# A streaming-encoder step: the last third of the projection moved into the attention's first tiles, and one chain of small passes for two DeltaNet tiles

## The chip, the cores and the metric

The kernel runs on one core of one Trainium2 chip. The metric is device time in microseconds (us); before the change three runs took 2844.42, 2846.88 and 2847.21 us (median 2846.88). Five engines work side by side, each on its own queue in order: TensorE (PE, with its weight loads as PEld), VectorE (DVE), ScalarE (ACT), GpSimd (POOL), and SyncE (SP), which here issues every DMA.

## The reference, cut to what matters

One layer of a streaming encoder over 2048 prompt frames and 8 running streams of 16 frames (17 tiles of 128 tokens). One input projection feeds three token mixers; an output projection, a layer norm and a feed-forward block follow.

```python
proj = jnp.einsum('btd,de->bte', x, lp['w_in'])
qa, ka, va, qkv_b, beta_in, a_in, gate_b, u_c = jnp.split(proj, split_points(IN_SIZES), axis=-1)
out_a = band_attention_prompt(qa, ka, va, lp['a_rel_bias'])     # softmax over 9 chunks of 64 keys
qb = l2_normalize(qb); kb = l2_normalize(kb)                    # x * rsqrt(sum(x*x) + 1e-6)
ob, s_new = gated_delta_rule(qb, kb, vb, g, beta, s0)           # group B, DeltaNet
ob = ob * lax.rsqrt(jnp.mean(ob * ob, -1, keepdims=True) + RMS_EPS) * lp['b_norm_w'] * gate
y_c, h_re, h_im = s5_ssm(u, ...)                                # group C, S5
mix = jnp.concatenate([out_a, out_b, out_c], axis=-1) @ lp['w_out']
x = layer_norm(DN_ALPHA * x + mix, lp['ln1_g'], lp['ln1_b'])
```

## The kernel before

Every float32 product of a projection is made of three matmuls of a rounded part and a rest (`mm3`, L64: high by high, low by high, high by low). Both parts come from `split` (L58): ACT casts, DVE subtracts.

The stages, in program order:

- **Projection 1** (`project1`, L263): the columns for S5, DeltaNet and the gates, half of the values, in three token parts, and keys, values and queries of the last 512 tokens and the streams.
- **Projection 2** (`project2_all`, L320): keys (two blocks of columns), second half of the values, queries (two blocks) for three blocks of 512 tokens: 15 steps. A step of keys or queries has 48 matmuls of 512 columns, the values' step 96 of 256 columns; one token block is 288 matmuls. Results go through a bank of `pps` (two), an ACT pass into `st` (two buffers), and a store to `kT`, `vS` or `qT` in DRAM.
- **DeltaNet** (`deltanet`, L166): tiles in pairs. For a tile `b_pre` runs the convolution, sums of squares `ss`, one reciprocal root by bit trick and three Newton rounds (`rsqrt`, L335: 12 DVE passes of 128x8), six factors `F`, and the products inside a chunk; `b_inverse` inverts the diagonal blocks of both tiles; then `b_solve`, `b_rec` (the state's recurrence) and `b_out`, which has a root of its own (12 passes of 128x4).
- **S5** (`s5`): eight steps with a round through DRAM each, then the gated output (`glw`).
- **Attention** (`attention`, L1070): setup, then 16 query tiles of four rounds (two heads each). Tile i looks at min(i+1, 5) key tiles, so the first tiles are short. A round is: scores on PE (`aps`), a DVE pass that adds the bias `nb` and takes the minimum, an ACT exponential, a DVE normalisation of `P`, transposes on PE into `tps` (three banks), copies to `PT`, and products with the values (`aob`). Tiles 1 to 8 also carry one running stream each (`sK`, `sV`).

`merge` (L121) interleaves generators: projection 2 at cost 1, DeltaNet at 1.0, S5 at 1.2 per step. Below that, a scheduler that models the engines orders each engine's instructions; a free engine takes what is ready, the earlier in the program first. With these paces DeltaNet and S5 are done when 10 of the 15 steps of projection 2 are, and the third token block (288 matmuls) runs with no partner. The attention's setup loads eight overlapping bias windows `rv` (L1084, two buffers, the tag `qd`) that ACT turns into `nb` (L1085); POOL then fills two corners (L1086, L1087). The query tile takes the same two buffers after them: `qd` (ACT, L1199, L1201) and its rest `qlz` (POOL, L1200).

Of the kernel before, what the change touches and what calls it, by code (L numbers as in the profile page):

```python
# [2 lines left out]

# [6 lines left out]
F32 = mybir.dt.float32  # L10
# [21 lines left out]
PACE1B = 1.25  # L32
PACE_B = 1.0
PACE_C = 1.2
KPITCH = 23 * 16

BLOCKS = ((0, 6), (6, 6), (12, 5))
# [4 lines left out]
class K:  # L42
# [31 lines left out]
    def run(self, upto=99):  # L74
        nc, A = self.nc, self.A
        with self.es:
            self.cst = self.pool("cst", 1)
            self.dram = self.pool("dram", 1, bass.MemoryType.DRAM)
            d = self.dram

            def parts(name, rows):
                return [d.tile([rows, T], F32, name=f"{name}{j}") for j, (_, T, _) in enumerate(PARTS)]

            self.bT = parts("bT", 768)
            TA = (512, 512, 512, 640)
# [12 lines left out]
            self.mixT = d.tile([1024, NT], F32, name="mixT")  # L98
            self.x1 = d.tile([NT, DM], F32, name="x1")
            self.x2 = d.tile([12 * 128, DM], F32, name="x2")  # L100
            self.wu0D = d.tile([7, 128, DM], F32, name="wu0D")
            self.ident = self.ld(self.cst, "c_ident")
            self.mix(upto)
            self.wes = ExitStack()
            self.w_load(self.wes)
            with ExitStack() as es:
                self.attention(es)
            if upto < 4:
                self.wes.close()
            if upto >= 4:  # L110
                with ExitStack() as fes:
                    self.w_out(fes)
                    if upto >= 5:
                        self.ffn(fes)
            for n in getattr(self, "debug", ()):
                o = A["dbg_" + n]
                t = getattr(self, n)
                nc.sync.dma_start(o, t[t.shape[0] - o.shape[0]:])
# [9 lines left out]
            except StopIteration:  # L128
                now.remove(s)

    def mix(self, upto):
        nc, A = self.nc, self.A
        bes, ses = ExitStack(), ExitStack()
        self.bp = self.pool("bp", 3, PSUM, es=bes, side="right")
        self.brp = self.pool("brp", 1, PSUM, es=bes, side="right")
        self.pp = self.pool("pp", 2, PSUM, es=ses)
        self.s5p = self.pool("s5p", 2, PSUM, es=ses)
        self.flip = 0
        self.parts_done = 0
        deltanet = self.deltanet()  # L140
        self.s5c = self.pool("s5c", 1, es=ses)
        with ExitStack() as es:
            dense = self.project1(es)
            next(dense)
            self.s5_setup()
            for _ in range(5):
                next(dense)
            self.parts_done = 1
            self.b_consts(bes)
            self.b_pools(bes)  # L150
            due = 0.0
            for i, _ in enumerate(dense):
                if i in (5, 11):
                    self.parts_done += 1
                due += PACE1 if i < 12 else PACE1B
                while due >= 1:
                    next(deltanet)
                    due -= 1
        with ExitStack() as es:
            self.merge((self.project2_all(es), 1.0), (deltanet, PACE_B), (self.s5(), PACE_C))  # L160
        nc.sync.dma_start(A["o_k"], self.kT[3])
        nc.sync.dma_start(A["o_v"], self.vS[3])
        ses.close()
        bes.close()

    def deltanet(self):  # L166

# [5 lines left out]
        for t in [0, 2, 4, 6, 8, 10, 16, 12, 14]:  # L173
            n = 1 if t == 16 else 2
            while not ready(t + n - 1):
                yield 0.1
            if gates < min(t // 6, 2):
                gates += 1
                self.b_gates(gates)
            blk = self.bw.tile([32 * n, 16, 16], F32, name="blk", tag="blk", bufs=2)  # L180
            st = []
            for i in range(n):
                st.append(self.b_pre(t + i, blk, i))
                yield 1
            TU = self.b_inverse(st, blk)
            for x, (T, U) in zip(st, TU()):
                self.b_solve(x, T, U)
                o = self.bw.tile([128, 1, 4, 64], F32, name="o", tag="o", bufs=2)
                if t == 16:
                    self.b_rec_sample(x, o)  # L190
                else:
                    self.b_rec([x], o)
                self.b_out(x["t"], 1, o)
                yield 1
        self.nc.sync.dma_start(self.A["o_sp"], self.S)

    def evac(self, dst, src, scale=None):
# [273 lines left out]
    def t2(self, name, tag="pa"):  # L471
        return self.bw.tile([128, 4, 128], F32, name=name, tag=tag, bufs=5 if tag == "pa" else 1)

    def b_pre(self, t0, blk, bi):

        nc, A = self.nc, self.A
        V, mm = nc.vector, nc.tensor.matmul
# [40 lines left out]
        elif t0 + n == 16:  # L518
            nc.sync.dma_start(A["o_cvp"], cv[:, :, 0])
        qk = bw.tile([128, n, 8, 64], F32, name="qk", tag="qk", bufs=2)  # L520
        ss = bw.tile([128, n * 8], F32, name="ss", tag="ss", bufs=2)
        R = []
        for i in range(n):
            t = t0 + i
# [9 lines left out]
            for f in range(2):  # L534
# [2 lines left out]
            V.tensor_tensor(r[:, :, 0:64], ps[:, 0:256].rearrange("p (h d) -> p h d", h=4),  # L537
                            self.hbeta[:, t].unsqueeze(2).to_broadcast([128, 4, 64]), OP.mult)
            R.append(r)
        V.tensor_scalar(ss, ss, 4e-6, None, OP.add)  # L540
        rn = self.rsqrt(bw, ss, n * 8, "bn").rearrange("p (t h) -> p t h", h=8)
        F = bw.tile([128, n, 6, 4], F32, name="F", tag="F", bufs=2)
# [4 lines left out]
        V.tensor_tensor(F[:, :, 3], F[:, :, 1], self.beta[:, tt], OP.mult)  # L547
        V.tensor_tensor(F[:, :, 4], F[:, :, 3], self.egc[:, tt], OP.mult)
        V.tensor_tensor(F[:, :, 5], F[:, :, 1], self.kd[:, tt], OP.mult)
        st = []  # L550
        for i in range(n):
            t = t0 + i
# [206 lines left out]
        for p in range(2):  # L759
            nc.sync.dma_start(A["o_ss"][:, p], Sc[p])  # L760

    def b_out(self, t0, n, o):

        nc = self.nc
        V = nc.vector
        bw, bp = self.bw, self.bp
        T = n * 128
        of = o.rearrange("p t h e -> p (t h) e")
        sq = bw.tile([128, n * 4, 64], F32, name="osq", tag="po", bufs=4)
        nc.gpsimd.tensor_tensor(sq, of, of, OP.mult)  # L770
        ms = bw.tile([128, n * 4], F32, name="ms", tag="ms", bufs=2)
        V.tensor_reduce(ms, sq, AX.X, OP.add)
        V.tensor_scalar(ms, ms, 1.0 / 64, 1e-6, OP.mult, OP.add)
        rn = self.rsqrt(bw, ms, n * 4, "on")
        V.tensor_tensor(sq, of, rn.unsqueeze(2).to_broadcast([128, n * 4, 64]), OP.mult)
        g = bw.tile([128, 2, T], F32, name="gt", tag="po", bufs=4)
        gsrc, gs = self.at(self.gT, t0)
# [292 lines left out]
    def attention(self, es):  # L1070
# [1 line left out]
        c = self.pool("ac", 1, es=es, side="right")  # L1072
        self.ak = self.pool("ak", 2, es=es, side="right")
        self.asp = self.pool("asp", 4, PSUM, es=es, side="right")
        self.sc = self.pool("sc", 1, es=es)
        self.sw = self.pool("sw", 1, es=es)
        self.aw = self.pool("aw", 2, es=es)
        self.atp = self.pool("atp", 3, PSUM, es=es)
        self.aop = self.pool("aop", 1, PSUM, es=es)
        nb = self.nb = c.tile([128, 8, 640], F32, name="nb", tag="nb")  # L1080
        r = A["relrev"]
        for h in range(8):
# [20 lines left out]
        t = self.a_tile(0)  # L1103
        for q in range(2):
            self.a_queries(t, q)


        rounds = []
# [3 lines left out]
        for i in range(16):  # L1112
# [3 lines left out]
            for p in range(4):  # L1116
# [31 lines left out]
                    self.s_turn(sample)  # L1148
                if p == 3 and i >= 8:
                    self.w_part(i - 8)  # L1150
            t = t1
            if i == 8:
                nc.sync.dma_start(self.mixT[0:512, SEQ:NT].rearrange("(f p) t -> p f t", p=128), self.sos)
# [6 lines left out]
        h, l = (w0[:, i].bitcast(F32R) for i in (1, 2))  # L1160
        self.w_in(0, w0[:, 0], self.y0, h, l)
        self.w_tile(0, self.y0, h, l, lambda: self.asp.tile([128, 512], F32, name="aps", tag="s"))

    def tsplit(self, parts, t):
        src, sl = self.at_a(parts, t)
# [74 lines left out]
    def a_turn(self, s):  # L1240
# [2 lines left out]
        units = s["units"] = [(q, j) for j in range(s["nk"]) for q in range(2)]  # L1243
        for u in range(0, len(units), 4):
            m = units[u:u + 4]
            ps = self.atp.tile([128, 512], F32, name="tps", tag="t")
            for k, (q, j) in enumerate(m):
                self.nc.tensor.transpose(ps[:, k * 128:(k + 1) * 128], P[:, q, j * 128:(j + 1) * 128], self.ident)
            src = ps[:, 0:len(m) * 128].rearrange("p (k t) -> p k t", t=128)
# [80 lines left out]
    def s_turn(self, s):  # L1330
        nc = self.nc
        P = s["P"]
        PT = s["PT"] = self.aw.tile([128, 10, 128], F32, name="sPT", tag="PT")
        ps = self.atp.tile([128, 512], F32, name="tps", tag="t")
# [3 lines left out]
        ps = self.atp.tile([128, 512], F32, name="tps", tag="t")  # L1338
# [15 lines left out]

    def s_out(self, b, s):

        ps = self.atp.tile([128, 512], F32, name="tps", tag="t")
# [577 lines left out]
```

## Time and profile before

| | us |
|---|---|
| median of three runs (2844.42 to 2847.21) | 2846.88 |
| the profiled execution | 2848.35 |
| its span | 2846.6 |
| PE busy | 2739.7 (96%) |
| DVE busy | 1947.2 (68%) |
| ACT, POOL busy | 1307.0, 1037.4 |

The span divides into projection 1 with DeltaNet (0 to 580), projection 2 with DeltaNet and S5 (to 867), projection 2 alone (to 918), attention (to 1205), and output projection and feed-forward. A busy time is the union of the instructions' durations; matmuls overlap, so their pitch is less than their duration. The PE clock of a stretch is a share of full speed.

### The profile page before, as it was taken

To read this page: it belongs to the slowest core of one execution; us is meant where nothing else is said; L and a number is where in the kernel's file an instruction comes from. 1 tells how busy PE (TensorE), PEld (TensorE's weight loads), DVE (VectorE), ACT (ScalarE), POOL (GpSimd) and SP (SyncE) were. 2 spreads that over 40 slices of the span, in tenths; PEclk is the share of its full clock that TensorE was granted. 3 is DMA by queue.
4 is the path that set the end of the run, shared out by engine and by line. 5 is a ranking of instruction groups with operands and counts; after the bars stand their busy time and mean duration, and the time that the engine had idled before them with its cause. 6 is when DMAs were issued, how large, how long until landed. Compare 5 with 4: busy or idle time off the path is not lost.

```text
span 2846.6 us, 46363 instructions
## 1 busy us (share of the span) xinstructions
PE 2739.7 (96%) x16685; PEld 2405.9 (85%) x16685; DVE 1947.2 (68%) x4949; ACT 1307.0 (46%) x2714; POOL 1037.4 (36%) x914
## 2 busy tenths in 40 slices
PE   8999999989989899999999999999999999999998
PEld 8988888867777677788889998989999988998897
DVE  7587888798653788878755555566556557676676
ACT  3554554343355778612334433454434335444443
POOL 0010111232221232122354454445544553676674
PEclk9999999999999999999999999999999999999999
DMA  5734445555457652156622211253222224422321
GB/s 183 208 106 118 116 114 125 151 147 155 146 147 244 207 168 61 51 199 203 231 88 65 84 60 60 74 207 119 74 74 90 89 67 165 155 91 94 119 87 55
DMA packets 293437, 355.55 MB, mean 125 GB/s; under 512 B 85699, under 2 KB 218647, under 8 KB 292887
## 3 DMA queue, kind: packets, MB, share of 16 engines
q1 hardware_dynamic: 293206, 352.59, 39.6%
q8 instruction: 131, 2.15, 0.3%
q14 instruction: 100, 0.81, 0.1%
HBM read 280.25 MB, written 74.89 MB: 125 GB/s over the span
## 4 chain that ended last, share of the span: by engine, by line
PE 71%; DVE 12%; DMA 6%; issue 4%; ACT 3%; POOL 3%; SPq 1%; DVEq 0%; ACTq 0%; POOLq 0%
PE fdp L66 8%; PE fdp L67 8%; PE fdp L65 8%; PE pps L66 3%; PE pps L67 3%; PE pps L65 3%; PE wops L65 2%; PE wops L67 2%; PE wops L66 2%; PE fupv L67 2%; PE fupv L65 2%; PE fupv L66 2%; PE fupz L67 2%; PE fupz L65 2%; PE fupz L66 2%
## 5 line engine op out<-in xcount | busy, mean ns | idle before, releaser
L1570 POOL TENSOR_TENSOR wu<-wur,wu 128x512 fp32r<-128x512 f32 x308 | 416.9, 1357 | 600.6 <-ACT wu L1569 599.6
L1693 DVE TENSOR_TENSOR fy<-fy,fdp 128x512 f32<-128x512 f32 x500 | 341.1, 685 | 255.8 <-PE fdp L67 255.6
L65 PE MATMUL fdp<-wdh,hh 128*128 128x512 f32 x1020 | 397.8, 391 | 1.6 <-DVE fy L1693 1.1
L67 PE MATMUL fdp<-wdh,hl 128*128 128x512 f32 x1020 | 397.3, 389 | 1.1 <-DVE hl L1643 1.1
L66 PE MATMUL fdp<-wdl,hh 128*128 128x512 f32 x1020 | 397.2, 389 | 0.8 <-DVE wdl L61 0.8
L1569 ACT CAST wu<-wur 128x512 fp32r<-128x512 f32 x308 | 189.5, 617 | 427.1 <-DMA wur<-in_w_upL 173.5
L65 PE MATMUL pps<-xh,wh 128*128 128x384 f32 (+2 forms) x800 | 280.4, 352 | 11.7 <-ACT xh L60 10.4
L66 PE MATMUL pps<-xl,wh 128*128 128x384 f32 (+2 forms) x800 | 279.9, 350 | 2.1 <-DVE xl L61 2.1
L67 PE MATMUL pps<-xh,wl 128*128 128x384 f32 (+2 forms) x800 | 277.6, 348 | 0.1
L65 PEld LDWEIGHTS fdp<-wdh,hh 128*128 128x128 f32 x1020 | 191.4, 188 | 42.0 <-DVE fy L1693 2.8
L67 PEld LDWEIGHTS fdp<-wdh,hl 128*128 128x128 f32 x1020 | 191.5, 188 | 41.8 <-DVE hl L1643 2.0
L66 PEld LDWEIGHTS fdp<-wdl,hh 128*128 128x128 f32 x1020 | 191.5, 188 | 39.0 <-DVE wdl L61 1.1
L1643 DVE TENSOR_TENSOR hl<-fre,hh 128x384 fp32r<-128x384 f32 (+1 forms) x180 | 145.4, 809 | 83.9 <-ACT hh L1642 83.0
L60 ACT CAST wdh<-wdr 128x1024 fp32r<-128x1024 f32 x92 | 96.6, 1051 | 204.4 <-PE fdp L67 202.7
L65 PEld LDWEIGHTS pps<-xh,wh 128*128 128x128 f32 x800 | 152.1, 191 | 24.9 <-ACT xh L60 12.8
L61 DVE TENSOR_TENSOR wl<-wr,wh 128x512 fp32r<-128x512 f32 (+1 forms) x152 | 107.2, 714 | 87.0 <-ACT wh L60 84.5
L66 PEld LDWEIGHTS pps<-xl,wh 128*128 128x128 f32 x800 | 152.1, 190 | 13.8 <-DVE xl L61 5.1
L67 PEld LDWEIGHTS pps<-xh,wl 128*128 128x128 f32 x800 | 152.1, 190 | 11.4 <-issue 1.8
L61 DVE TENSOR_TENSOR wdl<-wdr,wdh 128x1024 fp32r<-128x1024 f32 x92 | 131.6, 1436 | 11.0 <-ACT wdh L60 10.9
L60 ACT CAST wh<-wr 128x512 fp32r<-128x512 f32 (+1 forms) x152 | 92.4, 619 | 79.8 <-DMA wr<-in_w_inA 35.0
L1638 ACT ACTIVATE fre<-fre,ld_b_up 128x384 f32<-128x384 f32 (+1 forms) x144 | 86.0, 597 | 65.3 <-DVE fre L1647 43.0
L1229 ACT ACTIVATE P<-P,st 128x640 f32<-128x640 f32 (+4 forms) x128 | 97.2, 760 | 30.5 <-DVE st L1226 29.8
(577 smaller groups left out, 7250.7 us busy)
## 6 DMA issues: line engine op xcount, KB each, us to landing
wdr<-in_w_dnL SPq DMA_DIRECT2D x96, 512.0 KB
wur<-in_w_upL SPq DMA_DIRECT2D x88, 512.0 KB
wr<-in_w_inA SPq DMA_DIRECT2D x70, 512.0 KB
TU<-tD SPq DMA_DIRECT2D x34, 256.0 KB
y<-in_x SPq DMA_DIRECT2D x17, 512.0 KB
x<-y SPq DMA_DIRECT2D x17, 512.0 KB
fxr<-x SPq DMA_DIRECT2D x17, 512.0 KB
fy<-x SPq DMA_DIRECT2D x17, 512.0 KB
```

Source lines behind the costliest of these rows:

```text
L60: nc.scalar.copy(hi, src)
L61: nc.vector.tensor_tensor(lo, src, hi.bitcast(F32), OP.subtract)
L65: mm(out, lh, rh, start=first, stop=False, **kw)
L66: mm(out, lh, rl, start=False, stop=False, **kw)
L67: mm(out, ll, rh, start=False, stop=last, **kw)
L1229: self.nc.scalar.activation(x, x, AF.Exp, scale=-1.0, bias=st[:, q:q + 1], accum_out=st[:, 2 + q:3 + q])
L1569: self.nc.scalar.copy(hi, src)
L1570: P.tensor_tensor(lo, src, hi.bitcast(F32), OP.subtract)
L1638: nc.scalar.activation(r, src, AF.Relu, bias=self.bu[:, c * 2 + i:c * 2 + i + 1])
L1643: V.tensor_tensor(hl, r, hh.bitcast(F32), OP.subtract)
L1693: V.tensor_tensor(y, y, ps[x], OP.add)
```

## The change

In `mix` only the first 10 steps of projection 2 are merged with DeltaNet and S5. Their pools are then closed, the attention (now a generator that yields after its setup and after each round) is started, and each of the five steps left is followed by three attention rounds. The attention's pools all move to the right-hand side of SBUF, the transposes have one PSUM bank until projection 2 is done, then two more. In `deltanet` a tile's `b_pre` is cut into `b_conv`, `b_factors` (once for a pair, passes of 128x16) and the rest; `b_out` is cut into `b_square` (per tile), `b_root` (once for a pair) and the rest.

```diff
+PACE_A = 3
@@ mix
         with ExitStack() as es:
-            self.merge((self.project2_all(es), 1.0), (deltanet, PACE_B), (self.s5(), PACE_C))
+            dense = self.project2_all(es)
+            self.merge((itertools.islice(dense, 10), 1.0), (deltanet, PACE_B), (self.s5(), PACE_C))
+            sps.close()
+            bes.close()
+            cs.close()
+
+            next(attention)
+            for _ in dense:
+                for _ in range(PACE_A):
+                    next(attention)
         nc.sync.dma_start(A["o_k"], self.kT[3])
         nc.sync.dma_start(A["o_v"], self.vS[3])
         ses.close()
-        bes.close()
+        self.atps.append(self.pool("atq", 2, PSUM, es=self.aes))
+        self.w_load(self.wes)
+        for _ in attention:
+            pass
@@ deltanet
+            st, qr = [], []
+            ss = self.bw.tile([128, n * 8], F32, name="ss", tag="ss", bufs=2)
             for i in range(n):
-                st.append(self.b_pre(t + i, blk, i))
-                yield 1
+                qr.append(self.b_conv(t + i, ss[:, i * 8:(i + 1) * 8]))
+                if i < n - 1:
+                    yield 1
+            F = self.b_factors(t, n, ss)
+            for i in range(n):
+                st.append(self.b_pre(t + i, *qr[i], F[:, i:i + 1], blk, i))
+                if i < n - 1 or n == 1:
+                    yield 1
             TU = self.b_inverse(st, blk)
-            for x, (T, U) in zip(st, TU()):
+            os_ = []
+            ms = self.bw.tile([128, n * 4], F32, name="ms", tag="ms", bufs=2)
+            for i, (x, (T, U)) in enumerate(zip(st, TU())):
...
-                self.b_out(x["t"], 1, o)
-                yield 1
+                os_.append((o, self.b_square(o, ms[:, i * 4:(i + 1) * 4])))
+                if i < n - 1:
+                    yield 1
+            rn = self.b_root(n, ms)
+            for i, (o, sq) in enumerate(os_):
+                self.b_out(t + i, 1, o, sq, rn[:, i * 4:(i + 1) * 4])
+            yield 1
@@ b_square, b_root (new; b_out loses these lines)
+    def b_square(self, o, ms):
+        sq = self.bw.tile([128, 4, 64], F32, name="osq", tag="po", bufs=4)
+        of = o.rearrange("p t h e -> p (t h) e")
+        self.nc.gpsimd.tensor_tensor(sq, of, of, OP.mult)
+        self.nc.vector.tensor_reduce(ms, sq, AX.X, OP.add)
+        return sq
+
+    def b_root(self, n, ms):
+        self.nc.vector.tensor_scalar(ms, ms, 1.0 / 64, 1e-6, OP.mult, OP.add)
+        return self.rsqrt(self.bw, ms, n * 4, "on")
@@ attention, a_turn, s_turn, s_out
-        self.atp = self.pool("atp", 3, PSUM, es=es)
+        self.atps = [self.pool("atp", 1, PSUM, es=es, side="right")]
...
+    def turn_bank(self):
+
+        self.turns += 1
+        pool = self.atps[-1] if self.turns % 3 else self.atps[0]
+        return pool.tile([128, 512], F32, name="tps", tag="t")
```

The first place is SP, where S5's output has been stored (`mixT<-oc`) and the bias windows `rv` are loaded, with the stores of the third block's keys (`kT<-st`) and the weights (`wr`). Before:

```order
L1065 DMA mixT<-oc_10612 128x2176
L249 DMA kT_69<-st 128x512
L210 DMA wr<-in_w_inA 128x1024
L1084 DMA rv<-in_relrev 128x640
L249 DMA kT_69<-st 128x512
L1084 DMA rv<-in_relrev 128x640
L210 DMA wr<-in_w_inA 128x1024
```

After:

```order
L1110 DMA mixT<-oc_10252 128x2176
L276 DMA kT_69<-st 128x512 x2
L237 DMA wr<-in_w_inA 128x1024
L1132 DMA rv<-in_relrev 128x640 x2
L1333 DMA rvs<-in_relrev 16x528 x2
L1132 DMA rv<-in_relrev 128x640 x2
```

The first window still stands behind the second key store and a weight load; the eight windows now go out in pairs, with the streams' windows `rvs` between them and no store or weight.

The second place is PE, where the attention's first scores (`aps<-kst0,qd`) begin. Before:

```order
L66 MATMUL pps_11465<-xl70_11048,wh_11433 128x512
L67 MATMUL pps_11465<-xh70_11047,wl_11434 128x512
L1224 MATMUL aps_11628<-kst0_11563,qd_11605 128x192
L1225 MATMUL aps_11628<-kst0_11563,qlz0_11567 128x192
L1224 MATMUL aps_11633<-kst0_11563,qd_11605 128x192
```

After:

```order
L67 MATMUL pps_11209<-wl_11178,xh70_10798 128x256
L68 MATMUL pps_11209<-wh_11177,xl70_10799 128x256
L1280 MATMUL aps_10896<-kst0_10707,qd_10749 128x192
L1281 MATMUL aps_10896<-kst0_10707,qlz0_10711 128x192
L1280 MATMUL aps_10901<-kst0_10707,qd_10749 128x192
```

The first scores stood behind the last queries of the block (`pps` of 512 columns); now they stand behind its second value tile (256 columns), with 144 of the block's 288 matmuls still to come.

The third place is PE in tile 1, after its last scores of the second round (`aps<-kst0` with `qlz1`). Before:

```order
L1224 MATMUL aps_11785<-kst0_11563,qd_11669 128x256
L1225 MATMUL aps_11785<-kst0_11563,qlz1_11568 128x256
L1248 MATMUL tps_11800<-ld_c_ident_92,P_11749 128x128
L1336 MATMUL tps_11807<-ld_c_ident_92,sP_11727 128x128 x2
L1248 MATMUL tps_11800<-ld_c_ident_92,P_11749 128x128 x3
```

After:

```order
L1280 MATMUL aps_11129<-kst0_10707,qd_10937 128x256
L1281 MATMUL aps_11129<-kst0_10707,qlz1_10712 128x256
L66 MATMUL pps_11237<-wh_11163,xh00_10756 128x256
L67 MATMUL pps_11237<-wl_11164,xh00_10756 128x256
L68 MATMUL pps_11237<-wh_11163,xl00_10757 128x256
```

This is the first place at which matmuls of the projection (`pps`) stand among those of the attention; the last of the 144 stands just ahead of tile 3's first scores.

## Rows read from the trace of the kernel before

**Rows 1.** The page: busy time, share of the span and instructions of each engine.

```profile
PE 2739.7 (96%) x16685; PEld 2405.9 (85%) x16685; DVE 1947.2 (68%) x4949; ACT 1307.0 (46%) x2714; POOL 1037.4 (36%) x914
```

**Rows 2.** Windows: stretch, busy time (and count) by engine, PE clock, DMA.

```profile
140.00:760.00 620.00, 584.96 (x4303) 501.58 (x4302) 502.71 (x1894) 279.79 (x702) 126.73 (x189) 0.99 0.47 128
580.00:640.00 60.00, 47.41 (x337) 37.56 (x337) 55.31 (x194) 29.67 (x71) 25.24 (x30) 0.91 0.58 161
...
918.00:934.00 16.00, 11.49 (x66) 7.14 (x64) 9.25 (x44) 11.16 (x35) 5.38 (x8) 0.61 0.66 210
934.00:960.00 26.00, 23.86 (x245) 16.98 (x247) 17.37 (x70) 18.51 (x51) 4.55 (x9) 0.91 0.74 225
```

**Rows 3.** PE's waits from 140 to 760: sum, times, longest.

```profile
PE bps L535 <- DVE s L515: 4.9, 3, 3.8
PE bps L587 <- POOL qdkb L574: 4.4, 9, 2.0
PE bps L583 <- DVE qkn L572: 3.4, 4, 1.3
...
PE bps L583 <- DVE F L548: 0.6, 1, 0.6
...
PE brs L690 <- DVE vn L687: 0.3, 1, 0.3
```

**Rows 4.** Two of the small passes: count, shortest/median/longest ns.

```profile
L349 DVE TENSOR_TENSOR bns<-bns,bnh x51: 146/158/599, 137.0 to 664.3; 128x8 f32<-128x8 f32 x51
L349 DVE TENSOR_TENSOR ons<-ons,onh x51: 136/154/567, 206.2 to 759.2; 128x4 f32<-128x4 f32 x51
```

**Rows 5.** The same for a factor of F.

```profile
L548 DVE TENSOR_TENSOR F<-F,b_egc x17: 143/673/1026, 140.6 to 667.0; 128x4 f32<-128x4 f32 x17
```

**Rows 6.** DVE in order of time: start, duration, instruction.

```profile
204.14 0.16 DVE L345 TENSOR_SCALAR bnh<-ss 128x8 f32<-128x8 f32 x1
204.21 0.15 DVE L773 TENSOR_SCALAR ms<-ms 128x4 f32<-128x4 f32 x1
204.28 0.16 DVE L344 TENSOR_SCALAR bny<-bnt 128x8 int32<-128x8 int32 x1
```

**Rows 7.** PE in order of time, around the first scores; in brackets the idle before.

```profile
892.65 0.38 PE L65 MATMUL pps<-wh,xh 128*128 128x256 f32 x1 [0.89 <-ACT st L198]
...
918.14 0.25 PE L1224 MATMUL aps<-kst,qd 128*128 128x192 f32 x1
...
958.50 0.50 PE L1224 MATMUL aps<-kst,qd 128*128 128x512 f32 x1
```

**Rows 8.** SP in order of time: the first and third window.

```profile
874.52 0.57 SPq L1084 DMA_DIRECT2D rv<-in_relrev  x1
...
881.52 0.33 SPq L1084 DMA_DIRECT2D rv<-in_relrev  x1
```

**Rows 9.** ACT in order of time: four of the eight `nb`.

```profile
880.76 0.74 ACT L1085 ACTIVATE nb<-rv 128x640 f32<-128x640 f32 x1
...
886.63 0.74 ACT L1085 ACTIVATE nb<-rv 128x640 f32<-128x640 f32 x1 [0.52 <-DMA rv<-in_relrev]
...
897.38 0.74 ACT L1085 ACTIVATE nb<-rv 128x640 f32<-128x640 f32 x1 [3.09 <-DMA rv<-in_relrev]
...
905.57 0.74 ACT L1085 ACTIVATE nb<-rv 128x640 f32<-128x640 f32 x1 [2.90 <-DMA rv<-in_relrev]
```

**Rows 10.** SP: the sixth and seventh window's issue.

```profile
893.07 0.87 SPq L1084 DMA_DIRECT2D rv<-in_relrev  x2
```

**Rows 11.** POOL in order of time, the end of the setup.

```profile
906.37 0.52 POOL L1086 MEMSET nb<- 64x512 f32 x1 [90.33 <-ACT nb L1085]
906.92 0.52 POOL L1087 MEMSET nb<- 64x512 f32 x1
908.46 1.45 POOL L1200 TENSOR_TENSOR qlz<-qr,qd 64x512 fp32r<-64x512 f32 x1 [1.01 <-ACT qd L1199]
...
918.46 1.53 POOL L1279 TENSOR_SCALAR nbs<-rvs 128x528 f32<-128x528 f32 x1 [4.16 <-PE aps L1224]
```

**Rows 12.** Windows again, at the two stretches of half clock.

```profile
602.00:610.00 8.00, 4.88 (x12) 3.91 (x13) 7.90 (x16) 4.02 (x9) 3.99 (x4) 0.50 0.76 208
921.00:938.00 17.00, 13.25 (x72) 8.29 (x71) 9.34 (x40) 11.05 (x33) 3.69 (x7) 0.52 0.73 222
```

More of the change, by code (lines that the diff above doesn't have):

```diff
@@ L1 @@
-import math
+import itertools, math
 from contextlib import ExitStack
@@ L102, in run @@
             self.ident = self.ld(self.cst, "c_ident")
-            self.mix(upto)
             self.wes = ExitStack()
-            self.w_load(self.wes)
             with ExitStack() as es:
-                self.attention(es)
+                self.mix(upto, self.attention(es))
             if upto < 4:
@@ L129, in merge, with mix @@
                 now.remove(s)
-    def mix(self, upto):
+    def mix(self, upto, attention):
         nc, A = self.nc, self.A
@@ L136, in mix @@
         self.pp = self.pool("pp", 2, PSUM, es=ses)
-        self.s5p = self.pool("s5p", 2, PSUM, es=ses)
+        sps = ExitStack()
+        self.s5p = self.pool("s5p", 2, PSUM, es=sps)
         self.flip = 0
@@ L140, in mix @@
         deltanet = self.deltanet()
-        self.s5c = self.pool("s5c", 1, es=ses)
+        cs = ExitStack()
+        self.s5c = self.pool("s5c", 1, es=cs, side="right")
         with ExitStack() as es:
@@ L180, in deltanet @@
             blk = self.bw.tile([32 * n, 16, 16], F32, name="blk", tag="blk", bufs=2)
-            st = []
+            st, qr = [], []
+            ss = self.bw.tile([128, n * 8], F32, name="ss", tag="ss", bufs=2)
             for i in range(n):
-                st.append(self.b_pre(t + i, blk, i))
-                yield 1
+                qr.append(self.b_conv(t + i, ss[:, i * 8:(i + 1) * 8]))
[6 more added lines that the diff above has]
+                    yield 1
             TU = self.b_inverse(st, blk)
-            for x, (T, U) in zip(st, TU()):
+            os_ = []
+            ms = self.bw.tile([128, n * 4], F32, name="ms", tag="ms", bufs=2)
+            for i, (x, (T, U)) in enumerate(zip(st, TU())):
                 self.b_solve(x, T, U)
@@ L472, in t2, with b_conv @@
         return self.bw.tile([128, 4, 128], F32, name=name, tag=tag, bufs=5 if tag == "pa" else 1)
-    def b_pre(self, t0, blk, bi):
+    def b_conv(self, t0, ss):
         nc, A = self.nc, self.A
@@ L520, in b_pre @@
         qk = bw.tile([128, n, 8, 64], F32, name="qk", tag="qk", bufs=2)
-        ss = bw.tile([128, n * 8], F32, name="ss", tag="ss", bufs=2)
         R = []
@@ L539, in b_pre, with b_factors @@
             R.append(r)
+        return qk, R
+    def b_factors(self, t0, n, ss):
+        V, bw = self.nc.vector, self.bw
         V.tensor_scalar(ss, ss, 4e-6, None, OP.add)
@@ L549, in b_pre @@
         V.tensor_tensor(F[:, :, 5], F[:, :, 1], self.kd[:, tt], OP.mult)
+        return F
+    def b_pre(self, t0, qk, R, F, blk, bi):
+        nc = self.nc
+        V, mm = nc.vector, nc.tensor.matmul
+        n = 1
+        sam = t0 == 16
+        bw, bk, bp = self.bw, self.bk, self.bp
         st = []
@@ L760, in b_rec_sample, with b_out @@
             nc.sync.dma_start(A["o_ss"][:, p], Sc[p])
-    def b_out(self, t0, n, o):
+    def b_square(self, o, ms):
[7 more added lines that the diff above has]
+        return self.rsqrt(self.bw, ms, n * 4, "on")
+    def b_out(self, t0, n, o, sq, rn):
         nc = self.nc
@@ L768, in b_out @@
         of = o.rearrange("p t h e -> p (t h) e")
[L769 to L774, printed above, removed]
         V.tensor_tensor(sq, of, rn.unsqueeze(2).to_broadcast([128, n * 4, 64]), OP.mult)
@@ L1074, in attention @@
         self.asp = self.pool("asp", 4, PSUM, es=es, side="right")
-        self.sc = self.pool("sc", 1, es=es)
-        self.sw = self.pool("sw", 1, es=es)
-        self.aw = self.pool("aw", 2, es=es)
-        self.atp = self.pool("atp", 3, PSUM, es=es)
-        self.aop = self.pool("aop", 1, PSUM, es=es)
+        self.sc = self.pool("sc", 1, es=es, side="right")
+        self.sw = self.pool("sw", 1, es=es, side="right")
+        self.aw = self.pool("aw", 2, es=es, side="right")
+        self.aop = self.pool("aop", 1, PSUM, es=es, side="right")
+        self.aes = es
+        self.atps = [self.pool("atp", 1, PSUM, es=es, side="right")]
+        self.turns = 0
         nb = self.nb = c.tile([128, 8, 640], F32, name="nb", tag="nb")
@@ L1105, in attention @@
             self.a_queries(t, q)
+        yield
         rounds = []
@@ L1150, in attention @@
                     self.w_part(i - 8)
+                yield
             t = t1
@@ L1245, in a_turn @@
             m = units[u:u + 4]
-            ps = self.atp.tile([128, 512], F32, name="tps", tag="t")
+            ps = self.turn_bank()
             for k, (q, j) in enumerate(m):
@@ L1333, in s_turn @@
         PT = s["PT"] = self.aw.tile([128, 10, 128], F32, name="sPT", tag="PT")
-        ps = self.atp.tile([128, 512], F32, name="tps", tag="t")
+        ps = self.turn_bank()
         for j in range(4):
@@ L1337, in s_turn @@
         self.nc.scalar.copy(PT[:, 0:4], ps.rearrange("p (k t) -> p k t", t=128))
-        ps = self.atp.tile([128, 512], F32, name="tps", tag="t")
+        ps = self.turn_bank()
         self.nc.tensor.transpose(ps[0:16, 0:128], P[:, 512:528], self.ident)
@@ L1355, in s_out @@
     def s_out(self, b, s):
-        ps = self.atp.tile([128, 512], F32, name="tps", tag="t")
+        ps = self.turn_bank()
         self.nc.tensor.transpose(ps[:, 0:128], s["P"][:, 0:128], self.ident)
```

## The prediction

> **What bounds the kernel now.** I read the page's busy line first: PE is busy 2739.7 us of 2846.6 (96%), DVE 68% [rows 1]. So a change pays only where PE is idle, or where its clock is down. The windows show how much of that lies in the two stretches the change touches [rows 2]. In 140 to 760, where DeltaNet runs beside the projections, PE is busy 584.96 of 620: 35.0 us idle. DVE is busy 502.71, idle 117.3. In 580 to 640 inside it the clock is 0.91, which is 0.09 x 60 = 5.4 us lost, and DVE is busy 55.31 of 60. Where the attention begins, 918 to 934, PE is idle 4.5 us with a clock of 0.61; from 934 to 960 it is idle 2.1 us.
>
> Third, the waits of PE in 140 to 760. They begin with DVE's `s` (4.9 us) and end with `vn` (0.3). The 14 rows on DVE and the one on POOL's `qdkb` add up to 27.3 us. Of these the chain that leads through the factors `F` has three: `qdkb` 4.4, `qkn` 3.4, `F` 0.6, together 8.4 [rows 3].
>
> Last, the instructions in order of time around the attention's start: PE goes through the third token block without a hole until its first scores at 918.14 [rows 7], while SP, ACT and POOL prepare the bias beside it [rows 8 to 11]. That preparation is finished about 10 us before PE asks for it. So it costs nothing before the change, because 288 matmuls cover it.
>
> **Part B, the shared chains.** For each tile of a pair there were 1 + 12 passes for the root of `ss`, 6 for `F`, 1 + 12 for the root of `ms`: 32. A pair now makes one set: 8 pairs x 32 = 256 DVE passes go; the ones that stay are twice as wide. A small pass has a median of 154 to 158 ns [rows 4], a factor of `F` 673 ns [rows 5]. But passes that don't depend on each other start 0.07 us apart (204.14, 204.21, 204.28) although each lasts 0.15 to 0.16 [rows 6]. So I count 0.075 us each, and eight of the long `F` rows at the 0.6 that they hold the engine longer: 256 x 0.075 + 8 x 0.6 = 24 us of DVE freed. By durations it would be 256 x 0.155 = 40 us.
>
> DVE is not the bound, so freed time is no gain by itself. Bounds: below, nothing, since PE waits on DVE for other things; above, every idle microsecond of PE in the stretch and the clock too, 35.0 + 5.4 = 40. On the other side stands a new wait: both tiles' factors wait for the second tile's convolution and sums, so tile 0 of a pair starts its products later. I have no row of such a pair; the longest `qkn` wait is 1.3 us [rows 3], and eight pairs of that are +10. The value: half of the 8.4 us on the factors' chain goes (one of the two chains of a pair is left), −4.2. The rest of the waits, 27.3 − 8.4 = 18.9, and the 5.4 of clock, together 24.3, I let shrink as DVE's idle time grows: 24 on 117.3 is 20%, so −4.9. B = −9 us. It is nearer to 0 than to 40 because the waits that stay, on `s` above all, have no pass of these chains in their names.
>
> Rows 6 show these starts 0.07 us apart, and the sum goes by them. The Trainium skill, page "VectorE: DVE Perf Modes", section "The TRN2 errata — SBUF-src ops pay a fixed extra latency per instruction", says against this that each instruction pays a fixed latency between instructions, so that many small tiles pay it each time; its measured fixed term of about 150 cycles at 0.96 GHz is 0.156 us (an estimate by that page). By it the 256 passes would free 40 us and more, DVE's idle time would grow by a third, and B would be some −12 instead of −9. The durations of rows 4 agree with that price and the starts of rows 6 do not, where passes are independent; in a chain of dependent ones the duration counts.
>
> **Part A, the mixing.** No matmul goes or comes; 144 of the 288 of the third block move from in front of the first scores into tiles 1 and 2. They took 892.65 to 918.14 = 25.5 us [rows 7], and PE stood idle 0.89 before them, so the half that stays ahead ends at 892.65 − 0.89 = 891.8 (its start is set by S5's end and is left as it was). From there on PE has nothing until the first scores may start.
>
> When may they? All eight `nb`, the two corners of POOL, the windows of the streams and the query tile come first, since the query takes the two buffers that the windows had. Before, the windows went out at 874.52, 881.52, ... with stores and weights between them [rows 8], the `nb` ended 0.74 after 880.76, 886.63, 897.38, ..., 905.57 [rows 9], that is 906.3 for the last. A window that went out at 881.52 was read at 886.63, 5.1 us later [rows 8, 9]; one from 893.07 at 897.38, 4.3 [rows 9, 10]. Now the first still stands behind a store and a weight load, so `nb` 0 ends at 881.5 as before; then the windows go in pairs. The remaining turns of two buffers are three for windows 2 to 6 (a landing of 5.1, a pass of 0.74 and an allowance of 0.15 for the issue, 6.0 each): 881.5 + 18.0 = 899.5 for `nb` 6, and its partner at once behind, some 901 with the second pass and its wait for the shared queue. Behind that POOL's rows: two corners of 0.52 (now the last two stand behind each other), one pass of 1.53 for the streams' window, which stands ahead of `qlz`, and `qlz` of 1.45 [rows 11]: 1.0 + 1.5 + 1.5 = 4.0 from 901 is 905; the corners partly overlap the last pass, and I take 904. With landings of 4.3 it is 902.5; if the last `nb` comes at 906.3, as before, it is 910.3.
>
> So the new stall is 904 − 891.8 = 12.2 us. What it costs in the end is read at tile 3, from which on all is as before. Tile 3's first score was at 958.50, 40.4 us behind 918.14 [rows 7]. Now: 904 + 40.4 + 25.5 for the moved matmuls, less what they fill. They don't fill tile 0 and half of tile 1, as they stand on PE's queue behind the second round of tile 1; so of the idle 4.5 and 2.1 I count half or 3 us. 904 + 40.4 + 25.5 − 3 = 966.9, and 966.9 − 958.5 = +8.4. Bounds: with 902.5 and all 6.6 filled, +3.3; with 910.3 and 1 filled, +18.7. I take +8, for the row that it is nearest to is a landing of 5.1. The clock gives nothing back in this: 921 to 938 ran at 0.52, near the lower of the two levels, 1.2 GHz [rows 12], and a stall of 12 us comes ahead of the same tile now. That one transpose bank serves tiles 0 to 2 instead of three I cost at nothing, as those matmuls are few against the 25.5 us of dense ones that stand between; without that cover it is part of the upper bound.
>
> The stretch in which S5 ends gets the streams' two sample loads earlier, beside S5's own; I have no row that prices this and take 0.
>
> **Sum.** +8.4 − 9.1 = −0.7 us against the profiled 2848.35, which is 1.47 above the median 2846.88. Set against the median: 2846 us, no change. What counts as none is within 0.2%, 5.7 us, about what a measurement of this kernel can tell.
>
> **Rivals.** *Faster, by the dip at 602 to 610.* There the clock was 0.50 and PE busy 4.88 of 8 while DVE was busy 7.90 [rows 12], and all of 580 to 640 has DVE at 92% [rows 2]: here DVE is the bound. If freed passes undo this, its idle 12.6 us and the 5.4 of clock go nearly whole, and half the chain's waits (4.2) with them: B = −22. With A at +4 to +8 that is −14 to −18: about 2832. For it speaks that an engine at 92% with a queue in order turns each pass into delay; against it that the first of the waits, on `s`, is not on these chains. Chance 0.36.
>
> *Slower, by the setup.* The stall ahead of the first scores decides. If the windows come no faster than before (SP's queue still holds a store and a weight ahead of the first, and keys and values of the attention now land in the same microseconds), the last `nb` ends at 906.3, the scores begin at 910.3, the stall is 18.5 us and A = +15 to +18. With B at half its value, −4.5: +10 to +14, about 2859. It decides from A − B = 5.7 on, so with B = −9 from a first score at 910 on. For it speaks that SP issues in order, so that its first window waits where it did; against it that stores and weights have left the row of windows. Chance 0.26.
>
> *The mixing does nothing it says.* Half the block still stands in front, and the matmuls that were to fill tile 0 stand behind it, so A is only a shift of 25.5 us with a stall in its place. That is how I have it in the forecast; if the stall were filled as well, A = 0 and the time 2838, inside the faster side.
>
> **Chances.** Forecast (both terms within a few us of each other) 0.38, faster 0.36, slower 0.26. Its own range is 2841 to 2852; with the rivals' times 2832 and 2859, and a little of their own bounds, 2828 to 2862 holds 8 in 10. The extremes, B = −40 or A = +18.7 with B = +10, are left out.
>
> **What would show it.** A: PE idle of about 12 us between the last matmul of the values' second tile and the first score, named after `qlz`, `nb` or a window; first score at about 904 less what B gained by then; idle from there to tile 3 below 4 us outside the half clock. B: DVE some 24 us less busy in 140 to 760 (40 by durations), the rows on `F`, `qkn` and `qdkb` halved, PE's idle there at about 28 us. It is wrong if the stall is under 4 us, if 580 to 640 loses most of its 12.6 idle, or if new waits on tile 0's factors stand among the longest of PE.

## The result

The changed kernel took 2873.15 us (median of 4 runs, 2869.82 to 2880.28) against 2845.65 for the kernel before: ratio 1.0101, 95% interval 1.0086 to 1.0116, 27.5 us slower. (A difference here is that of the medians; a ratio is worked out from the single runs and can differ from it by a microsecond or two.) The forecast was 2846 with a range to 2862. It lies 11 us beyond the range, and 14 beyond the time of the slower rival. The profiled execution took 2880.28 us, the slowest of the four.

The page of the changed kernel, its first part (as [rows 1]):

```profile
PE 2751.1 (96%) x16685; PEld 2414.8 (84%) x16685; DVE 1939.6 (67%) x4693; ACT 1308.1 (45%) x2714; POOL 1039.5 (36%) x914
```

DVE has its 256 instructions less (4949 to 4693), and over the whole span that is 1947.2 − 1939.6 = 7.6 us of DVE, where the sum counted 24. The windows of the stretches of [rows 2]:

```profile
140.00:760.00 620.00, 571.44 (x4221) 492.17 (x4221) 477.76 (x1612) 270.44 (x685) 124.49 (x181) 0.98 0.44 122
580.00:640.00 60.00, 47.32 (x317) 37.41 (x317) 48.22 (x166) 27.55 (x66) 24.60 (x34) 0.91 0.44 133
```

From 140 to 760 PE is idle 48.6 us where it was 35.0, and its clock is 0.98 for 0.99: some 13.5 + 6 us lost. In 580 to 640 DVE is less busy (48.22 for 55.31), and PE's busy time (47.32 for 47.41) and clock are what they were. (The 25 us that DVE lacks in the long window are mostly not saved but late: the page's total fell by 7.6.)

Windows at the same times don't hold the same work: the long one has 4221 matmuls where it had 4303. The same work ends with S5's last gated matmuls (`glw`), before and after:

```profile
862.64 2.09 PE L1057 MATMUL s5p<-yq,glw 128*128 128x272 f32 x8
```
```profile
883.80 2.09 PE L1102 MATMUL s5p<-yq,glw 128*128 128x272 f32 x8
```

The windows up to there, before and after:

```profile
0.00:864.73 864.73, 806.23 (x5546) 703.31 (x5547) 655.93 (x2375) 397.75 (x952) 154.91 (x227) 0.99 0.51 144
```
```profile
0.00:885.89 885.89, 815.00 (x5550) 710.28 (x5551) 649.75 (x2120) 397.68 (x953) 158.70 (x231) 0.97 0.50 143
```

Of the 21.2 us more, 12.4 are idle time of PE (58.5 to 70.9) and 8.8 are matmuls that take longer, at a clock of 0.97 for 0.99.

PE's longest waits from 140 to 760, as [rows 3]:

```profile
PE s5p L1014 <- DVE WB L1009: 9.7, 1, 9.7
PE brs L831 <- DVE osq L820: 7.2, 6, 2.1
PE bqs L689 <- DVE R L701: 5.9, 9, 1.7
...
PE brs L776 <- DVE vns L784: 4.0, 1, 4.0
PE bps L623 <- DVE qkn L612: 3.0, 4, 0.9
...
PE bps L627 <- POOL qdkb L614: 0.6, 3, 0.2
```

The waits that the sum halved did shrink: `qdkb` from 4.4 to 0.6, `qkn` from 3.4 to 3.0, `F` from 0.6 to no row. What came instead has other names: the outputs' transposes (`osq`), the solve (`R`), the streams' recurrence (`vns`), S5 (`WB`). The wait on `WB` lies at 626, in the stretch 580 to 640, where PE's idle time is 12.7 us and was 12.6: there it takes the place of other waits and adds nothing.

The attention's start on PE, as [rows 7] (idle before in brackets), and tile 3's first score:

```profile
918.15 0.50 PE L1280 MATMUL aps<-kst,qd 128*128 128x192 f32 x1 [9.97 <-ACT qd L1257]
...
982.02 0.50 PE L1280 MATMUL aps<-kst,qd 128*128 128x512 f32 x1
```

The first score comes when it came before (918.14), with 144 matmuls still to do: S5's last gated matmuls came 21 us later. At tile 3 the lag is 982.02 − 958.50 = 23.5 us.

### The profile page after: what moved, and what is told of

Same layout as the page of the kernel before. It is cut to its first block, busy times and chain, and to the rows that moved or that the text cites. A ratio compares the mean times of both kernels' runs of the same rounds, so it can differ in the third digit from the quotient of the medians.

```text
span 2878.5 us, 46133 instructions
## 1 busy us (share of the span) xinstructions
PE 2751.1 (96%) x16685; PEld 2414.8 (84%) x16685; DVE 1939.6 (67%) x4693; ACT 1308.1 (45%) x2714; POOL 1039.5 (36%) x914
## 4 chain that ended last, share of the span: by engine, by line
PE 75%; DVE 10%; DMA 5%; issue 5%; ACT 4%; POOL 2%; SPq 1%; DVEq 0%; ACTq 0%; POOLq 0%
PE fdp L66 8%; PE fdp L67 8%; PE fdp L68 8%; PE pps L68 3%; PE pps L66 3%; PE pps L67 3%; PE fupv L68 2%; PE fupv L66 2%; PE fupv L67 2%; PE fupz L68 2%; PE fupz L67 2%; PE fupx L67 2%; PE fupx L68 2%; PE fupz L66 2%; PE fupx L66 2%
## 5 line engine op out<-in xcount | busy, mean ns | idle before, releaser
L68 PEld LDWEIGHTS pps<-xh,wl 128*128 128x128 f32 x800 | 152.4, 191 | 12.4 <-DVE wl L62 3.3
L225 ACT ACTIVATE st<-pps 128x384 f32<-128x384 f32 (+3 forms) x122 | 56.5, 466 | 119.3 <-PE pps L68 106.9
```

The lines of the kernel that those rows point to most:

```text
L68: mm(out, ll, rh, start=False, stop=last, **kw)
L225: self.nc.scalar.activation(dst, src, AF.Copy, scale=scale or 1.0)
```

## The experiments

Differences are against the kernel before on the same chip. "Order" and "slack", named in some expectations, are theories on the DeltaNet part that came up after the first four runs.

**1. The two halves apart.** DeltaNet's new functions in the kernel before:

```diff
-                st.append(self.b_pre(t + i, blk, i))
+                qr.append(self.b_conv(t + i, ss[:, i * 8:(i + 1) * 8]))
...
+            rn = self.b_root(n, ms)
```

> The kernel before with both shared chains and nothing else of the change. Theory 1 (the DeltaNet part of the change makes the loss ahead of the attention, the mixing the rest): +14 to +20 us against before, and S5's last gated matmul as late as in the changed kernel, some 21 us later than the 862.6 of before. Theory 2 (the loss ahead of the attention comes from the mixing: the pools on the other side and the sample loads beside S5): within 4 us of before. The prediction's own figure for this part was -9.

Measured +18.4 us (1.0059, 1.0046 to 1.0071). Next the changed kernel with the old DeltaNet functions (the same lines the other way).

> The changed kernel with the old DeltaNet code, so the mixing alone. Theory 1: +7 to +12 us against before (the prediction had +8), S5's last gated matmul within 3 us of before's 862.6, an idle stretch of PE of about 10 us ahead of the first score. Theory 2: +20 us or more, S5's end some 20 us late.

Measured +8.6 (1.0028, 1.0018 to 1.0037). S5's last gated matmuls, in the first and in the second:

```profile
880.67 2.09 PE L1092 MATMUL s5p<-yq,glw 128*128 128x272 f32 x8
```
```profile
865.50 1.08 PE L1077 MATMUL s5p<-yq,glw 128*128 128x272 f32 x4
```

The parts add up to 27.0 of 27.5: theory 1 holds. PE in the mixing alone, at the end of the dense half block, at the first scores and at tile 3's first score:

```profile
886.82 0.28 PE L68 MATMUL pps<-wh,xl 128*128 128x256 f32 x1
898.25 0.50 PE L1255 MATMUL aps<-kst,qd 128*128 128x192 f32 x1 [11.14 <-ACT qd L1232]
900.52 0.53 PE L1256 MATMUL aps<-kst,qlz 128*128 128x192 f32 x1 [1.78 <-POOL qlz L1231]
...
964.89 0.50 PE L1255 MATMUL aps<-kst,qd 128*128 128x512 f32 x1
```

12.9 us of stall in two rows; the sum had 12.2.

**2. The mixing's stall.** All eight windows land at once. Each has a place of its own, all loads go out ahead of the eight ACT passes, and the streams' windows behind them:

```diff
+        room = [nb[:, h + 4] for h in range(4)]
+        room += [self.aw.tile([128, 1024], F32, name="rv", tag="qd")[:, 0:640] for _ in range(2)]
+        rt = self.aw.tile([128, 10, 128], F32, name="rt", tag="PT").rearrange("p a b -> p (a b)")
+        room += [rt[:, 0:640], rt[:, 640:1280]]
-            rv = self.aw.tile([128, 1024], F32, name="rv", tag="qd")[:, 0:640]
+            rv = room[h]
...
+        for h in range(8):
+            rv = room[h]
```

> The mixing alone (old DeltaNet code), but the eight bias windows land in eight places (four in the slots of nb that are written later, two in the query's buffers, two in a PT buffer), so that no load waits for an earlier one. If the stall ahead of the first scores is made of the turns of two buffers and is what the mixing costs (+8.6): PE's idle there falls from 12.9 to under 5 us and the time to within 3 us of before. Rival (the moved matmuls fill nothing and cost themselves, whatever the stall): the stall shrinks but the time stays at +6 or more.

Measured −1.6 (0.9990, 0.9981 to 0.9999), 10 us below the mixing alone. The first score, and the last windows on SP (`rv`, `rt`):

```profile
890.39 0.33 PE L1261 MATMUL aps<-kst,qd 128*128 128x192 f32 x1 [1.74 <-ACT qd L1238]
```
```profile
873.57 1.13 SPq L1111 DMA_DIRECT2D rv<-in_relrev  x2
874.80 1.46 SPq L1111 DMA_DIRECT2D rt<-in_relrev  x2
```

So the turns of two buffers, with what was issued between them, were the stall. Yet with it gone the mixing gains only 1.6 us, and the interval barely excludes no change. One reason stands in tiles 4 to 8, from the same product with the values to the same: before, in the mixing alone, then here.

```profile
982.15:1091.25 109.10, 99.17 (x1053) 77.60 (x1052) 90.06 (x296) 82.89 (x185) 30.30 (x31) 1.00 0.48 149
```
```profile
989.29:1101.84 112.55, 100.02 (x1053) 78.01 (x1052) 94.13 (x297) 84.32 (x185) 29.60 (x31) 0.98 0.47 146
```
```profile
977.10:1092.10 115.00, 101.72 (x1054) 79.62 (x1053) 94.02 (x297) 84.26 (x185) 29.59 (x31) 0.97 0.46 143
```

The same matmuls take 5.9 us longer here, 3.4 in the mixing alone, at a lower clock. Why they do is open. Then `PACE_A` at 5:

> The mixing alone with the windows landing at once, and five attention rounds behind each of the five dense steps instead of three, so that the last dense matmuls fall into tiles 4 and 5, where PE was idle 10 us of 109. If dense work fills that idle time: 3 to 6 us below before. Rival (tiles 4 to 8 are paced by DVE at 90 us of 109 and the dense matmuls' own passes, and one transpose bank holds them longer): within 3 us of before, or slower.

Measured +3.5 (1.0013, 1.0003 to 1.0023), as the rival had it. Dense matmuls don't fill those tiles for free.

**3. Which chain.** One of the two shared at a time:

> The kernel before with the factors of a pair shared, the output's root per tile. Theory 1a (tile 0 of a pair starts its products only behind the second tile's convolution, which delays inverse and recurrence: waits on R, vn, vns): +8 to +18 us. Theory 1b (the shared root at the pair's end makes the loss): -6 to +3, the waits on osq as small as before (1 us).

> The kernel before with the output's root shared by a pair, the factors per tile. Theory 1b (both tiles' outputs wait for the second recurrence and one chain of small passes, and PE's transposes of osq stand in its queue meanwhile: 8.4 us of waits on osq in the changed kernel, 1.0 before): +8 to +18 us, with at least 6 us of waits on osq. Theory 1a: -6 to +3.

Factors alone (`b_conv`, `b_factors`, old `b_out`): +21.8 (1.0070, 1.0051 to 1.0088). Root alone (`b_square`, `b_root`, old `b_pre`): +14.0 (1.0041, 1.0029 to 1.0053). Both theories fail: one chain costs 21.8 or 14.0 where the two together cost 18.4, and PE's waits on `osq` from 140 to 867 are 9.4 us with the factors shared, where the root wasn't touched, and 7.9 with the root. The cause isn't in one chain.

**4. The order without the sharing, and the saving without the order.** The first edit, against the kernel with both chains shared:

```diff
-            F = self.b_factors(t, n, ss)
+            F = [self.b_factors(t + i, 1, ss[i]) for i in range(n)]
-            rn = self.b_root(n, ms)
+            rn = [self.b_root(1, m) for m in ms]
```

> The kernel before, with the DeltaNet steps cut and waiting as in the shared version (a pair's factors behind both convolutions, both outputs at the pair's end), but every tile keeps its own passes: nothing is shared, no pass is saved. Theory order (what costs is that the pair's work is moved together: the factors wait for the second tile, the outputs come in one lump with the next pair's inverse): +12 to +25 us, as the shared version (+18). Theory slack (what costs is that fewer passes are counted in the order that was written down, so that PE's transposes and products stand closer to the DVE passes they wait for than the chip can follow): at most +6.

Measured +17.4 (1.0059, 1.0046 to 1.0073), where the shared version had +18.4. No pass is saved and no tile waits for another's data. (Not shown above: the small passes have more buffers, two for each root's and four for `ss`, `ms` and `F`; `osq` of both tiles is held to the pair's end as in the shared version.) The program's order alone is enough for the cost. PE's waits on the factors in this kernel, 140 to 760:

```profile
PE bps L616 <- POOL qdkb L603: 2.7, 3, 2.2
...
PE bps L612 <- DVE qkn L601: 0.7, 2, 0.3
```

In the other run `range(3)` becomes `range(1)` in `rsqrt`:

> The kernel before with one Newton round instead of three in both reciprocal roots of DeltaNet: the last two rounds are left out, 12 DVE passes less per tile, 204 in all, and each chain about 1 us shorter; no step is moved. The prediction's reckoning of freed DVE time: -3 to -8 us. Theory slack: +5 to +15, with new waits on osq or F. Theory order: -5 to +2, waits on osq as small as before.

Measured +0.3 (1.0001, 0.9993 to 1.0010). Its page:

```profile
PE 2737.4 (96%) x16685; PEld 2400.7 (84%) x16685; DVE 1932.2 (68%) x4745; ACT 1306.5 (46%) x2714; POOL 1042.3 (37%) x914
```

15.0 us of DVE are freed, twice what the change freed, and the time stays. (Kernels with all 4949 passes lie between 1943.7 and 1951.8, so such differences are good to some microseconds.) Slack falls, and so does the reckoning behind half of part B: by the interval the gain is at most 2 us. Then one piece moved, tile 0's output behind the second recurrence:

```diff
-                self.b_out(x["t"], 1, o)
-                yield 1
+                outs.append((x["t"], o))
...
+            for to, o in outs:
+                self.b_out(to, 1, o)
```

> The kernel before, where the output of a pair's first tile is written behind the second tile's recurrence, with its own root: nothing shared, no new wait, one block of the program moved later. Theory order (the place of the outputs in the program costs, not the shared chain): +8 to +18, as the shared root alone (+14). Rival (only the wait of both outputs for one root costs): within 4 us of before.

Measured +14.9 (1.0051, 1.0036 to 1.0066): order again.

**5. Can other cuts mend it?** The shared chains with the `yield` between the convolutions moved behind the second tile's products, then with eight half steps (`PACE1`, `PACE1B` doubled, `PACE_B` halved):

> The kernel before with both shared chains, but the steps cut so that a pair's both convolutions, its factors and tile 0's products stand in the first step, as early as before; inverse and first recurrence begin the third step again. Theory order, in the form that the products stand too late in the program: 0 to +8. In the form that the outputs in one lump at the pair's end cost (the shared root alone cost +14): +10 to +16. Theory slack: +12 or more.

> Both shared chains, but a pair is cut into eight half steps at twice the pace, so that the dense matmuls are spread evenly over its pieces: convolution, convolution, factors and products of tile 0, products of tile 1, inverse, first recurrence, second recurrence, outputs. Theory lumps (the steps of the changed kernel are of uneven size, a convolution alone in the first and products, inverse and recurrence in the third): 0 to +6. Theory order (inside a pair the pieces follow each other in the costly order, whatever the cuts): +12 or more.

Measured +22.9 (1.0078, 1.0064 to 1.0091) and +15.6 (1.0056, 1.0036 to 1.0075). Neither early products nor even steps mend it.

**6. The old DeltaNet code at other paces.** One constant changed each time:

```diff
-PACE1 = 2
+PACE1 = 1.75
```

> The kernel before with DeltaNet's pace in projection 1 at 1.75 in place of 2 steps for each dense step: the same instructions and waits, other places in the program. Theory tuned (any other order of the DeltaNet work costs as much, since the order before was fitted to its steps): +8 or more. Theory order (what costs is the order inside a pair): within 6 us of before.

> The kernel before with DeltaNet's pace in projection 1 at 2.25 in place of 2. Theory tuned (the DeltaNet steps and the paces of before fit each other, and moving the work either way costs): +6 or more. Rival (1.75 cost +15 only because it made DeltaNet later): within 4 us of before, or faster.

> The kernel before with the pace of the third token part at 1.5 in place of 1.25; everything ahead of it stays. Theory tuned: +3 or more. Rival: within 3 us of before.

Measured +15.0 at 1.75 (1.0048, 1.0033 to 1.0063), +25.7 at 2.25 (1.0091, 1.0076 to 1.0106), and +10.9 with the third part at 1.5 (1.0040, 1.0025 to 1.0055). "Tuned" holds and "order", as a matter of the order inside a pair, fails. The same for the shared chains:

> Both shared chains with the pace in projection 1 at 2.25: DeltaNet's steps, which stand later in the program in the shared version, come earlier again. Theory late (the shared version only comes too late against the dense steps, so that S5 ends 18 us late): +4 to +10 in place of +18. Theory tuned: +12 or more.

> The same with a pace of 2.5. Theory late: 0 to +8, less than at 2.25 or as much. Theory tuned: anywhere from +8 to +25, with no trend from 2 over 2.25 to 2.5.

+31.1 (1.0110, 1.0095 to 1.0125) and +12.6 (1.0043, 1.0026 to 1.0060): 18, 31, 13 at 2, 2.25 and 2.5, no trend.

## Why the prediction was wrong

**Part A came near its number, in part by luck.** Forecast +8.4, measured +8.6 for the mixing alone. Its main step was right: a stall of 12.2 forecast and 12.9 in two rows, and taking the turns of two buffers away took 10 us off. But both ends of the stall came some 4.5 us sooner than in the sum, and these errors cancel. The dense half ended at 887.1 and not 891.8, although S5 ended 3 us later than before; and the last `nb` of the mixing alone ended at 896.5 and not 901, as the second, third and fourth pair of windows went out at 881.25, 885.81 and 890.32, 4.5 us apart and not 6.0:

```profile
895.75 0.74 ACT L1108 ACTIVATE nb<-rv 128x640 f32<-128x640 f32 x1 [1.57 <-DMA rv<-in_relrev]
```

From the first score to tile 3's it took 964.89 − 898.25 = 66.6 us, where 40.4 + 25.5 is 65.9: the 3 us counted as filled idle time were not filled. Tiles 4 to 8, which I took to be "as before", lost 3.4 us. Two slips move nothing: the upper bound with 910.3 and 1 filled is +16.7, not +18.7, and "A − B = 5.7" has to be A + B.

**Part B failed, in the step "the rest of the waits shrinks as DVE's idle time grows" and in what stood on its other side.** The part forecast −9.1 and measured +18.4.

- The waits on the factors, 8.4 us [rows 3], did become 3.6 in the changed kernel, but not for the reason given. In the order alone, where no chain is left out, they are 3.4: the new order moved them.
- The freed DVE time was too large, 24 against 11.4 (1947.2 less 1935.8 on the page of the chains alone; 7.6 in the changed kernel), probably because many removed passes ran beside others. By their durations it would have been 40, further off.
- More to the point, freed DVE time is worth next to nothing here: 15.0 us freed without moving a step changed the time by 0.3. The −4.9 was worked out by proportion from a busy share, and a share of time has no wait in it.
- The other side was priced as one new data wait, tile 0 for tile 1's convolution, at most +10, and none of it went into the sum. The loss isn't that wait: the same order without any sharing costs +17.4. The outputs, which the change moves to the pair's end, had no term at all, and moving the first of them alone costs +14.9. I treated the moved steps as if only their data mattered; they also change what stands ahead of what on five queues in order.

None of the three signs that were to show the forecast wrong came: the stall is there, 580 to 640 keeps its idle time, and the waits on the factors are smaller than before. Of the signs for part B two came, but by accident: DVE 25 us less busy in 140 to 760, since the work was late, and the smaller waits on the factors. PE's idle time there, to fall to 28 us, rose to 48.6.

How such a loss looks, on PE and in the windows of the changed kernel:

```profile
451.33 1.16 PE L689 MATMUL bqs<-R,CT 128*128 128x128 f32 x8 [0.83 <-ACT CT L698]
454.17 2.07 PE L689 MATMUL bqs<-R,CT 128*128 128x128 f32 x8 [1.68 <-DVE R L701]
```
```profile
448.00:452.00 4.00, 3.17 (x28) 3.03 (x28) 3.86 (x18) 2.05 (x5) 0.25 (x1) 1.00 1.08 289
452.00:462.00 10.00, 8.32 (x46) 8.04 (x45) 6.89 (x16) 3.71 (x9) 4.02 (x8) 0.66 0.60 151
```

Two steps of a solve stand behind each other on PE with nothing dense between them. PE waits 0.83 and 1.68 us, and the clock of 452 to 462 is 0.66, partly at the lower level of 1.2 GHz: 0.34 x 10 = 3.4 us more. And a wait on `osq` in the same kernel, DVE in order of time, behind it the transpose on PE:

```profile
431.00 0.68 DVE L62 TENSOR_TENSOR wl<-wr,wh 128x512 fp32r<-128x512 f32 x1
431.60 0.15 DVE L375 TENSOR_TENSOR ons<-onz 128x8 f32<-128x8 f32 x1
431.68 0.75 DVE L667 TENSOR_TENSOR Ti<-Ti,tp 64x60 f32<-64x60 f32 x1
432.35 0.15 DVE L376 TENSOR_TENSOR ons<-ons,onh 128x8 f32<-128x8 f32 x1
432.43 0.68 DVE L62 TENSOR_TENSOR wl<-wr,wh 128x512 fp32r<-128x512 f32 x1
...
434.66 0.75 DVE L820 TENSOR_TENSOR osq<-o,onz 128x256 f32<-128x256 f32 x2
```
```profile
435.22 0.41 PE L831 MATMUL brs<-ld_c_ident,osq 128*128 128x128 f32 x2 [1.38 <-DVE osq L820]
```

The root's chain is short in itself, but these steps of it stand each behind a pass of 0.7 us of the next pair's inverse or of the dense weights (`wl`), and PE's transposes were written too close behind it. That the splitting passes are the general cause is not shown: at pace 1.75 there are 12 of them (`wl`, `xl`) inside its 17 such chains, in the kernel before 20 inside 17, and yet it is slower.

**What is shown, and what stays open.** The kernel before behaves like a fitted point: twelve kernels that place DeltaNet's work otherwise, five of them without the shared chains and three of these by a single constant, are all slower by 11 to 31 us. The 18 us of the shared chains lie inside that band, so the chains themselves have no price that these runs can tell from that of a new order. Which feature of the old order does it is open. No wait is common to the slow kernels: the longest names are `WB` (9.7) and `osq` (7.2) in the changed one, `s` (6.9 us) in the order alone, `qdkb` (11.1) at pace 2.25. Nor does every other order lose: with one Newton round the instructions stand in another order too, at no cost.

What the loss is made of is alike, though. The windows up to S5's end in the order alone and at pace 1.75:

```profile
0.00:880.32 880.32, 813.61 (x5546) 707.89 (x5547) 666.47 (x2375) 397.55 (x952) 153.16 (x227) 0.98 0.50 141
```
```profile
0.00:879.83 879.83, 811.75 (x5545) 704.74 (x5546) 654.97 (x2375) 395.09 (x949) 162.40 (x224) 0.98 0.50 141
```

Against the 864.73 of before these are 15.6 and 15.1 us more: 8.2 and 9.6 of idle time on PE and 7.4 and 5.5 of longer matmuls, at a clock of 0.98 for 0.99. In the chains alone (880.67 + 2.09 = 882.76) it is 14.9 and 3.2. So a part of what a new order costs, up to half, stands in no wait but in slower matmuls; the forecast counted a lower clock in 580 to 640 alone.

The rivals: the slower one had the setup's stall as its cause and a time of 2859; the stall is there, but as forecast, and the further 18 us are not its. The faster one, by the dip at 602 to 610, is refuted by its own sign: from 580 to 640 DVE is less busy (48.22), and PE's idle time stayed at 12.7 and its clock at 0.91. With one Newton round, too, PE is idle 11.5 us there at 0.91.

The best kernel is the mixing with windows landing at once and the old DeltaNet code: 0.9990 of the kernel before and 29 us below the changed one.

## What to carry to other kernels

Where one engine is 96% busy and the others stand in queues whose order a planner wrote, price a moved step by a trial of moves that change nothing else (a pace, a `yield`): if those cost 11 to 26 us, a saving of a few microseconds off the critical engine must not be counted at its own size. Free time on an engine that isn't the bound is worth only the waits that end on it, row by row. And before moving cover away from a setup, count the buffer turns of its loads: here two buffers for eight loads were hidden behind 288 matmuls and cost 10 us when half of these left.

## What was not expected of the hardware

In the changed kernel a pause of PE of 0.83 us and one of 1.68, some 3 us apart and with nothing but a solve's small matmuls between them, came with 10 us at a clock of 0.66: 3.4 us lost, where the pauses themselves are 2.5. So here the pauses cost more than their own length. Which ones do is not shown, and their sum doesn't tell: in 580 to 640 PE is idle 12.6 to 12.7 us in the kernel before, the chains alone and the mixing alone, and the clock is 0.91, 0.88 and 0.89.
